# Four zs pairs beside the attention, silu written with tanh and a GpSimd multiply, split queries stored by row

## The chip, the core and the metric

One NeuronCore of a Trainium2 chip runs the whole kernel. The metric is the device time of one launch in microseconds. Five instruction queues work side by side, each strictly in its own order: PE (TensorE, matrix products), DVE (VectorE), ACT (ScalarE), POOL (GpSimd) and SP (SyncE, which only issues DMAs here). An instruction waits for others through semaphores, and whatever stands behind it on its queue waits with it.

## What is computed

The reference is one layer of a hybrid encoder on 1024 tokens of width 1024, in float32, cut here to what matters:

```python
h = rmsnorm(x, norm_g)
q, k, v, za, u, vs, zs, gm = split(h @ w_in)
q, k = partial_rope(q), partial_rope(k)
a   = (window_sink_attention(q, k, v, sinks) * silu(za)) @ w_att_out
sgo = chunked_spatial_gating(gelu(u), gelu(vs), ...)      # gelu(u) * (mixed + bias)
sgo = (sgo * silu(zs)) @ w_sg_out
ga, gs = split(sigmoid(gm + b_merge))
x = rmsnorm(x + (ga * a + gs * sgo) @ w_o, final_g)
```

The attention has 16 query heads and 2 key heads of 64 dimensions, a window of 128 frames in chunks of 64, and rotates the first 16 dimensions of each head. The change concerns `silu(zs)`, its product with the spatial gating's output, the rotation of q, and the order in which column groups of `h @ w_in` are computed.

## The kernel before

**Products.** Activations stand transposed: channels on the 128 partitions, tokens along the free dimension. Each float32 number is split into a high and a low part (`split`, L146: a copy on ACT makes `hi`, a subtraction on DVE makes `lo`), and a product is the sum of three matmuls, hi·hi, hi·lo and lo·hi. `gemm_pair` (L348) makes a pair of 128-channel groups `m` and `m+1` for all 1024 tokens with a seven-product scheme: seven calls of `product` (L331), 12 matmuls of 128x512 each. Their names in the profile are those of the activation forms: b11, t1, t2, b21, t3, b22, t4, in this order. Copies on ACT (L357, L361, L364) keep intermediate sums in tiles of the tag "x" (five buffers), additions on DVE (L369, L374, L378) finish three of the four 128x512 quarters there, and the fourth quarter is left in PSUM with its sign turned. After each quarter `gemm_pair` calls `finish(i, half, q, src, sign)`, and between products it calls a `hook`, seven times a pair.

**Weights.** `jobs` (L408 to L417) lists the pairs in the order in which their weights are loaded, summed (four additions on DVE, L240 to L243, for jobs made by `pair_job`) and split; `split_next` does this a few products ahead of use. The list has to be in the order in which the pairs are computed. For some later jobs the sums are made in DRAM ahead of time by accumulating DMAs on POOL's queue (`early_job`, L294, and `o_sums`, L440).

**Stages.** After the normalisation and the vs projection come: four u pairs, with `mix` (L763) beside them, which makes the spatial gating's output, multiplies it by gelu(u) (L783) and stores it in `s1_dr`; one pair for k and v; four q pairs; the zs pair 0 beside the last rotation steps; the zs pairs 2, 4 and 6 and then eight pairs for the merge gates (gs, ga), all eleven beside the attention; then za, the two output projections and the last product.

**Queries.** For each quarter of q, `split_q` (L878) makes hi and lo scaled by -1/8 and stores them in `q_hl`, shaped (2, 1024, 1024): hi or lo, row, token. A row's 512 tokens of hi and of lo lie in two places of 2 KB. `rotate` (L932) loads the rotating rows back from `q_raw`, turns them and overwrites them in `q_hl` by four DMAs for each half of the rotation. `query_stage` (L1027) loads, for a group of heads and 128 tokens, hi and lo by one DMA each.

**The zs pairs.** `zs_pair` (L1047) collects the four quarters, and only after the whole pair does silu on ACT (L1064) for all four, one behind the other by manual dependencies and behind the last exp (`exps`), and then multiplies each by its part of `s1_dr` on DVE (L1074) and stores it in `s_dr`. The parts are loaded into two tiles: of tag "rot" and after the pair for pair 0, of tag "g" from the third hook on for the others. So the four "x" tiles of a pair stay taken until these stores have landed, and the next pair takes three more.

**The order of the work.** A scheduler places each engine's instructions in a fixed order from the written order and its own estimate of times; `after` (L156) adds order without a wait. `part_of_attention` (L1250) advances the attention at each hook by one or two parts (`PARTS`, nine parts to a pair, seven in the first pair). A part is one of: scores and softmax (`softmax_stage`, L1092: matmuls L1110, minimum L1118 and L1119 on DVE, exp L1123 and L1133 on ACT, scaling L1141 on DVE and L1143 on ACT), turning the weights (`weight_stage`, L1146: transposes L1154, casts and subtractions) and the product with the values (`value_stage`, L1178: matmuls L1195, L1201 on ACT, L1202 on DVE, a store by POOL, L1204).

Of the kernel before, what the change touches and what calls it, by code (L numbers as in the profile page):

```python
# [30 lines left out]
P = 128  # L31
# [21 lines left out]
def hybrid_tile(  # L53
# [709 lines left out]
    def mix(g, half, q):  # L763

        pm = bank("tp")
        for t in range(4):
            nc.tensor.matmul(  # L767
                pm[:, t * P : (t + 1) * P],
                xh[:, half * 4 + t, g * P : (g + 1) * P],
                bias[-1][1][:, g % 4, :],  # L770
                start=True,
                stop=True,
            )
        p3 = pm[:].rearrange("p (t i) -> p t i", t=4)
        nc.vector.scalar_tensor_tensor(
            p3,
            p3,
            lg_sb[:, g : g + 1],
            bias[-1][0][:, g % 4, :].unsqueeze(1).broadcast_to([P, 4, P]),
            op0=ALU.mult,  # L780
            op1=ALU.add,
        )
        nc.vector.tensor_mul(q[:], q[:], pm[:])  # L783
        put(s1_dr, g, half, q[:])

    def both():
# [103 lines left out]

    halves = [slice(half * 64, half * 64 + 64) for half in range(2)]

# [39 lines left out]
    def rotate(g, pause):  # L932
# [7 lines left out]
        def split_rows(src, j):  # L940
# [1 line left out]
                src,  # L942
                [
                    (
                        (halves[half], a),
                        q_hl[a].rearrange("(h d) t -> h d t", h=16)[
                            8 * g : 8 * g + 8, 8 * j : 8 * j + 8, half_of(half)
                        ],
                    )
                    for a in range(2)  # L950
                    for half in range(2)
                ],
            )
# [23 lines left out]
    for m in range(0, KC, 2):  # L977

        def finish(i, half, q, src, sign):
# [4 lines left out]
            split_q(q[:], [(slice(0, P), q_hl[:, rows, half_of(half)].rearrange("a p t -> p a t"))])  # L984

        if m == 2:
            steps_of_q.append(rope_tables())
# [39 lines left out]
    def query_stage(g, t, par):  # L1027
# [1 line left out]
            key_stage(g, t)  # L1029
        qt = mtile([P, 4, P], F32R, "q", 2, aheads)  # L1030
        for j in range(2):
            rows = q_hl[j].rearrange("(c r d) t -> r d c t", r=2, d=HD)[par]
            nc.sync.dma_start(
                qt[j * HD : (j + 1) * HD].bitcast(F32), rows[:, 4 * g : 4 * g + 4, t * P : (t + 1) * P]
            )
        return qt

    qT = []
    exps = []

    def first_loads():
        for n in range(2):
# [1 line left out]
            yield  # L1044


    def zs_pair(m, hook, *place, ahead_by=0):  # L1047
        quarters, fetched, hooked = [], [], [0]

        def fetch(i, half):  # L1050
            fetched.append(get(s1_dr, m + i, half, *place))

        def step():
            hook()
            hooked[0] += 1
            if hooked[0] == ahead_by:
                for at in ((0, 0), (1, 1)):
                    fetch(*at)

        gemm_pair(hb, lambda *quarter: quarters.append(quarter), step)  # L1060

        first = None
        for i, half, q, src, sign in quarters:
            silu = nc.scalar.activation(q[:], src, AF.Silu, scale=sign)  # L1064
            first = first or silu
            if silu is not first:
                after(silu, first)
            elif exps:
                after(silu, exps[-1])
        for i, half, q, src, sign in quarters:  # L1070
            if not fetched:
                fetch(i, half)
            g = fetched.pop(0)
            nc.vector.tensor_mul(q[:], q[:], g[:])  # L1074
# [17 lines left out]
    def softmax_stage(g, t, par, qt):  # L1092
# [40 lines left out]
        exps.append(nc.scalar.activation(es[:], es[:], AF.Exp))  # L1133
# [123 lines left out]
        for _ in range(1 if first else PARTS[of_pair[0] % 7]):  # L1257
            next(parts, None)

    for m in range(2, KC, 2):  # L1260
        zs_pair(m, lambda: part_of_attention(m == 2), 2, ahead_by=3)
    for dst in (gs_dr, ga_dr):
        for m in range(0, KC, 2):
            gemm_pair(hb, rest(dst, m), part_of_attention)
    for _ in parts:
        pass
# [436 lines left out]
```

## Time and profile before

| what | value |
|---|---|
| median of 3 runs | 928.03 us (928.03 to 928.74) |
| the profiled execution's own time | 928.07 us |
| its span in the trace | 926.3 us, so 1.77 us lie around it |
| DVE busy over the span | 690.2 us |
| ACT busy over the span | 530.2 us |
| POOL busy over the span | 126.8 us |
| mean granted TensorE clock | 0.997 of full speed |

The profile names an engine, a source line, the tile written and the tiles read, the shape, and the duration. In a timeline row the first number is the start in us from the start of the span and the second the duration. What stands in square brackets is the idle time of that engine just before, and what ended it. In the table of stretches each row is a stretch of the span; after its length stand the busy times of the engines in it, with instruction counts in brackets, then the granted clock, the busy share of the DMA engines and GB/s. A busy PE is not PE at its peak: matmuls of one product start every 0.227 us, although each is shown with some 0.39 us.

### The profile page before, as it was taken

The numbers are of one execution on the slowest core, as the hardware profiler recorded it, in microseconds if no ns is written. First come the engines' busy times: TensorE is split into PE (matmuls) and PEld (weight loads), VectorE is DVE, ScalarE is ACT, GpSimd is POOL, SyncE is SP. The second block draws the span as 40 slices with busy tenths as digits, with TensorE's granted clock in tenths as the row PEclk, the third lists the DMA queues.
The fourth block names the chain that finished last, engine by engine and source line by source line (L and its number), as shares of the span: only waits on it lengthen the run. The fifth ranks groups of instructions, "written<-read, shape, count | busy, mean of one in ns | idle before, by whom it ended". The sixth has DMA issues, their size and how long they took to land.

```text
span 926.3 us, 13222 instructions
## 1 busy us (share of the span) xinstructions
PE 906.1 (98%) x4337; PEld 751.3 (81%) x4337; DVE 690.2 (75%) x1243; ACT 530.2 (57%) x1056; POOL 126.8 (14%) x189
## 2 busy tenths in 40 slices
PE   8999999999999989999999999999999999999996
PEld 5888888888888778778888888888887887888885
DVE  6874776656678678888878888746498589579996
ACT  7852433334444468887766676744475475467443
POOL 0002222213011001101111121001100111210012
PEclk9999999999999999999999999999999999999998
DMA  7328778887788777778787779779669765998632
GB/s 261 137 89 210 215 195 180 157 161 219 240 286 262 216 242 200 214 212 232 188 228 258 234 168 262 209 263 324 212 197 330 257 196 157 289 316 283 207 114 114
DMA packets 128972, 202.23 MB, mean 218 GB/s; under 512 B 12456, under 2 KB 60840, under 8 KB 128904
## 3 DMA queue, kind: packets, MB, share of 16 engines
q1 hardware_dynamic: 109752, 148.69, 49.1%
q0 software_dynamic: 19008, 52.44, 24.0%
q8 instruction: 34, 0.56, 0.2%
q14 instruction: 34, 0.28, 0.1%
q10 hardware_dynamic: 144, 0.26, 0.1%
HBM read 144.59 MB, written 86.11 MB: 249 GB/s over the span
## 4 chain that ended last, share of the span: by engine, by line
PE 74%; DVE 11%; DMA 7%; ACT 3%; issue 3%; SPq 1%; DVEq 0%; ACTq 0%
PE ps_mm L339 31%; PE ps_o L339 22%; PE ps_mm L595 4%; DVE wl L154 3%; PE ps_sc L339 2%; PE ps_tp L339 2%; PE ps_sc L1110 2%; PE ps_o L1195 2%; PE ps_tp L1154 2%; DMA wr<-in_w_dram 1%; PE ps_tp L564 1%; PE ps_sc L564 1%; PE ps_o L564 1%; PE ps_mm L564 1%; PE ps_tp L767 1%
## 5 line engine op out<-in xcount | busy, mean ns | idle before, releaser
L153 ACT CAST wh<-s 128x1024 fp32r<-128x1024 f32 (+1 forms) x78 | 78.2, 1005 | 95.3 <-PE ps_mm L339 44.7
L154 DVE TENSOR_TENSOR wl<-wr,wh 128x1024 fp32r<-128x1024 f32 (+1 forms) x80 | 75.7, 947 | 56.4 <-ACT wh L153 55.5
L153 ACT CAST wh<-wr 128x1024 fp32r<-128x1024 f32 (+1 forms) x80 | 66.3, 830 | 79.8 <-PE ps_mm L339 37.8
L154 DVE TENSOR_TENSOR wl<-s,wh 128x1024 fp32r<-128x1024 f32 (+1 forms) x78 | 90.9, 1166 | 12.1 <-ACT wh L153 12.1
L339 PE MATMUL ps_o<-T_b22h,wh 128*128 128x512 f32 x148 | 58.8, 398 | 1.7 <-ACT x L361 1.7
L339 PE MATMUL ps_o<-T_t1h,wh 128*128 128x512 f32 x148 | 59.2, 400 | 0.3 <-ACT wh L153 0.2
L339 PE MATMUL ps_o<-T_b22l,wh 128*128 128x512 f32 x148 | 57.8, 391 | 0.0
L339 PE MATMUL ps_o<-T_b22h,wl 128*128 128x512 f32 x148 | 57.8, 390 | 0.0
L339 PE MATMUL ps_o<-T_t1h,wl 128*128 128x512 f32 x148 | 57.7, 390 | 0.0
L339 PE MATMUL ps_o<-T_t1l,wh 128*128 128x512 f32 x148 | 57.7, 390 | 0.0
L339 PE MATMUL ps_mm<-T_b11h,wl 128*128 128x512 f32 x140 | 54.8, 392 | 2.1 <-DVE wl L154 2.1
L339 PE MATMUL ps_mm<-T_t4h,wh 128*128 128x512 f32 x140 | 55.2, 394 | 1.5 <-DVE x L374 0.8
L339 PE MATMUL ps_mm<-T_t2h,wh 128*128 128x512 f32 x140 | 54.9, 392 | 1.3 <-ACT x L357 1.2
L339 PE MATMUL ps_mm<-T_t3h,wh 128*128 128x512 f32 x140 | 55.4, 396 | 0.2 <-ACT x L364 0.2
L1123 ACT ACTIVATE pr<-ps_sc,sm 128x192 f32<-128x192 f32 (+2 forms) x128 | 50.9, 409 | 8.1 <-DVE sm L1119 7.1
L339 PE MATMUL ps_mm<-T_b11h,wh 128*128 128x512 f32 x140 | 55.0, 393 | 0.0
L339 PE MATMUL ps_mm<-T_t4h,wl 128*128 128x512 f32 x140 | 54.7, 391 | 0.0
L339 PE MATMUL ps_mm<-T_t3h,wl 128*128 128x512 f32 x140 | 54.7, 390 | 0.0
L339 PE MATMUL ps_mm<-T_b11l,wh 128*128 128x512 f32 x140 | 54.6, 390 | 0.0
L339 PE MATMUL ps_mm<-T_t2h,wl 128*128 128x512 f32 x140 | 54.6, 390 | 0.0
L339 PE MATMUL ps_mm<-T_t4l,wh 128*128 128x512 f32 x140 | 54.5, 390 | 0.0
L339 PE MATMUL ps_mm<-T_t2l,wh 128*128 128x512 f32 x140 | 54.5, 390 | 0.0
(352 smaller groups left out, 2403.9 us busy)
## 6 DMA issues: line engine op xcount, KB each, us to landing
wr<-in_w_dram SPq DMA_DIRECT2D x86, 256.0 KB
sums<-in_w_dram POOLq DMA_DIRECT2D x20, 512.0 KB, 5.6
s<-sums SPq DMA_DIRECT2D x20, 512.0 KB
s_dr<-x SPq DMA_DIRECT2D x32, 256.0 KB
q_hl<-qhl SPq DMA_DIRECT2D x16, 512.0 KB
q<-q_hl SPq DMA_DIRECT2D x64, 128.0 KB
wr<-in_w_dram SPq DMA_DIRECT2D x14, 512.0 KB
y_dr<-x POOLq DMA_DIRECT2D x28, 256.0 KB, 6.6
```

Source lines behind the costliest of these rows:

```text
L153: nc.scalar.copy(hi, src)
L154: return nc.vector.tensor_sub(lo, src, hi.bitcast(F32))
L339: nc.tensor.matmul(acc, lt, rt, start=fresh and k == 0 and n == 0, stop=k == 3 and n == 2, skip_group_check=True,)
L564: mm = nc.tensor.matmul(acc, lt, rt, start=k == 0 and n == 0, stop=k == KC - 1 and n == 2)
L595: nc.tensor.matmul(acc[:], lt, rt, start=k == 0 and n == 0, stop=k == KC - 1 and n == 2)
L767: nc.tensor.matmul(pm[:, t * P : (t + 1) * P], xh[:, half * 4 + t, g * P : (g + 1) * P], bias[-1][1][:, g % 4, :], start=True, stop=True,)
L1110: nc.tensor.matmul(sc[:, i, k0:], q_of[:, c, i * P : (i + 1) * P], kt[:, f, k0:], start=f == 0, stop=f == 1,)
L1123: nc.scalar.activation(held_in[c, i], sc[:, i, lo:hi], AF.Exp, bias=nmax[:, c, i : i + 1], scale=-1.0, accum_out=sums[:, c, i : i + 1],)
L1154: nc.tensor.transpose(dst, pr[:, i, block * P : block * P + width], ident[:])
L1195: nc.tensor.matmul(po[:, cs], lt, rt, start=n == 0, stop=n == len(terms) - 1)
```

## The change

- The job list moves the first gs pair (`W_SG`, m = 0) ahead of the zs pairs. The gs pair 0, with the plain `rest` finish (L462), now stands beside the rotation; the four zs pairs, then gs 2, 4 and 6 and the four ga pairs stand beside the attention: eleven pairs, as before.
- `silu(z) * s1` is written as `(tanh(z/2) + 1) * (z * s1/2)`. The factor 0.5 goes into the multiplication that makes s1: L783, a two-tensor multiplication, becomes a scalar-tensor-tensor instruction.
- `zs_pair` handles each quarter as soon as it is there. For three quarters GpSimd multiplies `src` into the loaded part `g`; for the fourth, which lies in PSUM, DVE does it. Then ACT makes tanh in place over the quarter, DVE adds one and multiplies by `g`, and the result is stored. The tanh writes over what GpSimd reads, so it waits for GpSimd. Two parts are loaded at the pair's first hook, and each finish loads one more, into two tiles of tag "g".
- The manual order of silu behind exp (`exps`) is gone.
- `q_hl` becomes (row, half of the tokens, hi or lo, 512), so that a row's hi and lo lie side by side in 4 KB. A half of the rotation stores by two DMAs instead of four.

```diff
     q_raw = scratch("q_raw")
-    q_hl = scratch("q_hl", (2, D, S))
+    q_hl = scratch("q_hl", (D, 2, 2, HALF))
...
-    for base, step in ((W_U, 1), (W_Q, 0), (W_ZS, 1), (W_SG, 2), (W_ATT, 2)):
+    ALL = range(0, KC, 2)
+    for base, step, ms in ((W_U, 1, ALL), (W_Q, 0, ALL), (W_SG, 2, ALL[:1]), (W_ZS, 1, ALL), (W_SG, 2, ALL[1:]), (W_ATT, 2, ALL)):
...
-        nc.vector.tensor_mul(q[:], q[:], pm[:])
+        nc.vector.scalar_tensor_tensor(q[:], q[:], 0.5, pm[:], op0=ALU.mult, op1=ALU.mult)
...
         for at, dst in places:
-            nc.sync.dma_start(dst, hl[at].bitcast(F32))
+            nc.sync.dma_start(dst, hl[at].rearrange("p a t -> p (a t)").bitcast(F32))
...
-            rows = q_hl[j].rearrange("(c r d) t -> r d c t", r=2, d=HD)[par]
+            rows = q_hl[:, t // 4, j].rearrange("(c r d) t -> r d c t", r=2, d=HD)[par]
...
+    steps_of_q += [rotate(1, 1), first_loads()]
+    gemm_pair(hb, rest(gs_dr, 0), part_of_q)
+    stage.close()
...
+        def finish(i, half, q, src, sign):
             g = fetched.pop(0)
-            nc.vector.tensor_mul(q[:], q[:], g[:])
+            if sign < 0:
+                nc.vector.scalar_tensor_tensor(g[:], src, sign, g[:], op0=ALU.mult, op1=ALU.mult)
+            else:
+                nc.gpsimd.tensor_tensor(g[:], src, g[:], op=ALU.mult)
+            nc.scalar.activation(q[:], src, AF.Tanh, scale=0.5 * sign)
+            nc.vector.scalar_tensor_tensor(q[:], q[:], 1.0, g[:], op0=ALU.add, op1=ALU.mult)
             put(s_dr, m + i, half, q[:])
-
-    steps_of_q += [rotate(1, 1), first_loads()]
-    zs_pair(0, part_of_q, 5, "rot")
-    stage.close()
+            fetch()
+
+        gemm_pair(hb, finish, step)
...
-    for m in range(2, KC, 2):
-        zs_pair(m, lambda: part_of_attention(m == 2), 2, ahead_by=3)
-    for dst in (gs_dr, ga_dr):
-        for m in range(0, KC, 2):
+    for m in ALL:
+        zs_pair(m, lambda: part_of_attention(m == 0))
+    for dst, ms in ((gs_dr, ALL[1:]), (ga_dr, ALL)):
+        for m in ms:
             gemm_pair(hb, rest(dst, m), part_of_attention)
```

More of the change, by code (lines that the diff above doesn't have):

```diff
@@ L944, in split_rows @@
                     (
[L945 to L948, printed above, removed]
+                        halves[half],
+                        q_hl[:, half].rearrange("(h d) a t -> h d (a t)", h=16)[8 * g : 8 * g + 8, 8 * j : 8 * j + 8],
                     )
-                    for a in range(2)
                     for half in range(2)
@@ L983, in finish @@
             rows = slice((m + i) * P, (m + i + 1) * P)
-            split_q(q[:], [(slice(0, P), q_hl[:, rows, half_of(half)].rearrange("a p t -> p a t"))])
+            split_q(q[:], [(slice(0, P), q_hl[rows, half].rearrange("p a t -> p (a t)"))])
         if m == 2:
@@ L1044, in first_loads, with zs_pair, fetch @@
             yield
[L1047 to L1051, printed above, removed]
+    steps_of_q += [rotate(1, 1), first_loads()]
+    gemm_pair(hb, rest(gs_dr, 0), part_of_q)
+    stage.close()
+    def zs_pair(m, hook):
+        quarters = [(0, 0), (1, 1), (0, 1), (1, 0)]
+        fetched, hooked = [], [0]
+        def fetch():
+            if quarters:
+                i, half = quarters.pop(0)
+                fetched.append(get(s1_dr, m + i, half, 2))
         def step():
@@ L1055, in step @@
             hooked[0] += 1
[L1056 to L1072, printed above, removed]
-            g = fetched.pop(0)
-            nc.vector.tensor_mul(q[:], q[:], g[:])
+            if hooked[0] == 1:
+                fetch()
+                fetch()
+        def finish(i, half, q, src, sign):
+            g = fetched.pop(0)
+            if sign < 0:
[4 more added lines that the diff above has]
+            nc.vector.scalar_tensor_tensor(q[:], q[:], 1.0, g[:], op0=ALU.add, op1=ALU.mult)
             put(s_dr, m + i, half, q[:])
-    steps_of_q += [rotate(1, 1), first_loads()]
-    zs_pair(0, part_of_q, 5, "rot")
-    stage.close()
+            fetch()
+        gemm_pair(hb, finish, step)
     stage = ExitStack()
@@ L1132, in softmax_stage @@
         nc.vector.tensor_add(es[:], sk.unsqueeze(1).broadcast_to([P, 2, 2]), nmax[:])
-        exps.append(nc.scalar.activation(es[:], es[:], AF.Exp))
+        nc.scalar.activation(es[:], es[:], AF.Exp)
         nc.vector.tensor_add(es[:], es[:], sums[:])
@@ L1258, in part_of_attention @@
             next(parts, None)
-    for m in range(2, KC, 2):
-        zs_pair(m, lambda: part_of_attention(m == 2), 2, ahead_by=3)
-    for dst in (gs_dr, ga_dr):
-        for m in range(0, KC, 2):
+    for m in ALL:
+        zs_pair(m, lambda: part_of_attention(m == 0))
+    for dst, ms in ((gs_dr, ALL[1:]), (ga_dr, ALL)):
+        for m in ms:
             gemm_pair(hb, rest(dst, m), part_of_attention)
```

5 lines of the change are left out of this document (1 added, 4 removed).

## The prediction

> **What bounds the kernel now.** I began with the page: span, engines.
>
> ```profile
> span 926.3 us, 13222 instructions
> PE 906.1 (98%) x4337; PEld 751.3 (81%) x4337; DVE 690.2 (75%) x1243; ACT 530.2 (57%) x1056; POOL 126.8 (14%) x189
> ```
>
> PE is taken all the time, so a change that takes no matmul away can only gain where matmuls start late. The second view is the table of stretches, cut at the first b11 matmul of each pair.
>
> ```profile
> 297.08:318.10 21.02, 20.13 (x88) 15.98 (x86) 13.94 (x24) 10.79 (x16) 0.00 (x0) 1.00 0.73 229
> 318.10:345.72 27.62, 25.06 (x126) 20.17 (x125) 20.51 (x54) 15.94 (x50) 0.00 (x0) 1.00 0.73 233
> 345.72:373.30 27.58, 26.83 (x146) 22.64 (x145) 22.84 (x50) 22.63 (x57) 3.56 (x4) 1.00 0.77 210
> 373.30:401.00 27.70, 26.65 (x145) 22.14 (x144) 23.89 (x55) 23.25 (x59) 4.99 (x6) 1.00 0.85 224
> 401.00:429.07 28.07, 27.54 (x147) 22.37 (x145) 23.75 (x56) 22.86 (x59) 3.33 (x4) 1.00 0.81 221
> ...
> 506.44:532.58 26.14, 26.14 (x147) 22.62 (x146) 21.55 (x51) 18.64 (x54) 2.36 (x4) 1.00 0.69 220
> 532.58:558.71 26.13, 26.13 (x147) 22.61 (x145) 21.51 (x51) 18.61 (x54) 5.00 (x6) 1.00 0.82 180
> 259.00:278.04 19.04, 19.04 (x85) 15.77 (x84) 15.18 (x26) 9.14 (x14) 4.39 (x8) 1.00 0.82 272
> ```
>
> The rows are, in order: the pair beside the last rotation (zs 0), the first pair beside the attention (zs 2), zs 4, zs 6, gs 0 (which carries the silu of zs 6); then two undisturbed pairs beside the attention (ga 0 and 2) and one undisturbed pair without it (a q pair). Attention pairs with nothing in their way take 26.13 to 26.14 us, a bare pair takes 19.04. The clock is 1.00 in all of them. So the five pairs in question take 21.02 + 27.62 + 27.58 + 27.70 + 28.07 = 131.99 us. Without their waits they would take 19.04, then 25.06 for the first attention pair (it has seven attention parts instead of nine; I take its PE busy time), then three times 26.13: 122.5 us. **At most about 9.5 us, 1.0% of the kernel, lie in the stretch that the change touches.** The clearest late matmuls there, from the PE timeline:
>
> ```profile
> 315.20 0.50 PE L339 MATMUL ps_mm<-T_t4h,wh 128*128 128x512 f32 x1 [0.78 <-DVE x L374]
> ...
> 331.40 0.50 PE L339 MATMUL ps_o<-T_b22h,wh 128*128 128x512 f32 x1 [1.73 <-ACT x L361]
> ...
> 381.70 0.50 PE L339 MATMUL ps_mm<-T_t2h,wh 128*128 128x512 f32 x1 [0.91 <-ACT x L357]
> ```
>
> Next I asked each of them what its releaser had waited for. The largest one, at 331.40, from DVE, SP and ACT:
>
> ```profile
> 321.62 2.40 SPq L198 DMA_DIRECT2D rot<-s_dr  x4
> 326.67 0.69 DVE L1074 TENSOR_TENSOR x<-x,rot 128x512 f32<-128x512 f32 x1 [5.22 <-DMA rot<-s_dr]
> 327.39 3.42 SPq L455 DMA_DIRECT2D s_dr<-x  x4
> 330.75 0.60 ACT L361 ACTIVATE x<-ps_o 128x512 f32<-128x512 f32 x1 [3.36 <-DMA s_dr<-x]
> 331.73 1.28 ACT L1123 ACT_TABLE_LOAD   x1 [0.39 <-DMA s_dr<-x]
> ```
>
> The reader is to see a chain: zs 0 loads its four s1 parts only after the rotation, DVE waits 5.22 us for them, the stores start at 327.39, and only when one has landed is an "x" tile free for ACT's copy at 330.75, which PE needs. At 381.70 the copy L357 comes late because it stands on ACT behind a silu block with its table loads:
>
> ```profile
> L1064 ACT ACT_TABLE_LOAD x4 | 5.1, 1283 | 0.1
> L1123 ACT ACT_TABLE_LOAD x4 | 5.1, 1283 | 0.4 <-DMA s_dr<-x 0.4
> ...
> L1064 ACT ACTIVATE x<-x 128x512 f32<-128x512 f32 x12 | 7.1, 625 | 0.6 <-DVE x L374 0.5
> ```
>
> **The change part by part.** *The gs pair beside the rotation.* Its quarters are stored directly, so the chain from 321.62 to 331.40 goes: no s1 part is loaded in this pair, four plain stores take the place of four loads and four late stores on SP, and one copy with a sign on ACT (some 0.6 us) that of four silu and a table load. That frees 2.56 us of waiting in the first attention pair (27.62 - 25.06). What is late next there is the softmax's own start, with the table load of 1.28 us that the first exp still needs; I leave 0.5 us for it, bounds 0 and 2. The rotation pair's other wait stays:
>
> ```profile
> 312.05 0.69 DVE L959 TENSOR_TENSOR rot<-rot,tab 128x512 f32<-128x512 f32 x1 [0.78 <-DMA rot<-q_raw]
> ...
> 314.47 0.68 DVE L374 TENSOR_TENSOR x<-x,ps_mm 128x512 f32<-128x512 f32 x1
> ```
>
> The subtraction L374, which PE waits for at 315.20, stands behind four rotation instructions, and these behind the load of q_raw. The built program of the changed kernel has them in the same order. I leave 1.2 of the 1.98 us that this pair is longer than 19.04, bounds 0.2 and 2.
>
> *Queries by row.* The same bytes; a rotation half has two DMAs instead of four, so this pair and the one before lose eight issues on SP of about 0.6 us each (2.40 for four at 321.62), on a queue that is not the bound. No trace shows a 4 KB row, so its price lies between landing earlier than before (the rotation's loads, and L374 behind them, come earlier: a gain of at most the 1.2 us above) and, if the reads with the doubled row pitch are slower, a query load that holds PE; I take nothing, since bytes and issue order stay.
>
> *Silu by tanh.* The changed program's ACT order has 8 table loads instead of 15: none stands between exp and tanh. A zs pair's ACT work falls by 2 x 1.283 = 2.57 us; tanh is a pass over the same 128x512, taken at silu's 625 ns (the trace has no tanh; I bound it by L361's 0.60 us and by twice silu, 1.25; the upper end would give back 2.5 of ACT's 2.57 us). ACT goes from about 23 to 20.5 us of 26, so the late L357 copies should go. The "x" tiles are given back quarter by quarter, as in the gs and ga pairs, which show no such wait.
>
> *DVE's bill.* The rows:
>
> ```profile
> L775 DVE SCALAR_TENSOR_TENSOR ps_tp<-ps_tp,lg_sb,bias 128x512 f32<-128x512 f32 x16 | 11.9, 753 | 0.6 <-PE ps_tp L767 0.6
> ...
> L1074 DVE TENSOR_TENSOR x<-x,g 128x512 f32<-128x512 f32 x12 | 8.2, 691 | 7.1 <-DMA g<-s_dr 3.7 <-ACT x L1064 3.2
> ```
>
> A zs pair now has four instructions like L775 (0.75) and one from PSUM, taken as long as L1074 (0.69): 3.69 us, against 4 x 0.69 = 2.76 before. On top of a plain attention pair (21.5) that is 25.2 us of DVE in 26.13, 96%. That is the tightest place of the changed kernel. Making s1 with the factor 0.5 costs 16 x (0.75 - 0.69) = 1.0 us more on DVE beside the u pairs, where I count nothing: only the store to s1_dr follows, and beside pairs without attention DVE has room (15.18 of 19.04 us in the q pair); without that cover it would be the 1.0 us.
>
> *GpSimd's multiply.* Three per zs pair, twelve in all.
>
> ```profile
> L1546 POOL TENSOR_TENSOR g<-bq,bq 128x512 f32<-128x512 f32 x2 | 2.6, 1305 | 4.3 <-DVE bq L1541 3.9 <-issue 0.4
> ```
>
> At 1.3 us each this is 3.9 us on an engine that is busy for 3 to 5 us of such a pair. Behind it wait ACT's tanh, so every exp and cast behind tanh, and POOL's own DMAs (paced sums and the attention's stores, both off the path). Does it slow DVE? The only place of this trace where DVE and such a multiply are close:
>
> ```profile
> 9.00 1.28 POOL L582 TENSOR_TENSOR T_t1l<-T_t3h,T_t1h 128x512 fp32r<-128x512 f32 x1 [7.56 <-ACT T_t1h L581]
> ...
> 9.44 0.69 DVE L554 TENSOR_TENSOR T_b11l<-ps_tp,T_b11h 128x512 fp32r<-128x512 f32 x1 [0.31 <-ACT T_b11h L553]
> ...
> 10.87 1.22 DVE L154 TENSOR_TENSOR T_t1l<-T_t3h,T_t1h 128x1024 fp32r<-128x1024 f32 x1
> ```
>
> A DVE instruction with one input in PSUM ran at its normal length beside it; the next one with both inputs in SBUF began after it had ended. So the trace bounds the price of a multiply for DVE between 0 and its own 1.28 us, and does not decide. The Trainium skill, "SBUF — State Buffer", section "SBUF: two separate sides", speaks against this change: it says that GpSimd and a VectorE instruction with two SBUF inputs take one shared pair of ports in turn, each holding it for its whole length. The rows above agree with it without proving it; by it the sum would move towards the slow rival below.
>
> *Loading s1.* Two tiles, so the third part is loaded after the first finish, two products ahead of its use.
>
> ```profile
> 409.55 0.42 SPq L198 DMA_DIRECT2D g<-s_dr  x1
> ...
> 413.96 0.69 DVE L1074 TENSOR_TENSOR x<-x,g 128x512 f32<-128x512 f32 x1 [1.75 <-DMA g<-s_dr]
> ```
>
> A load takes 413.96 - 409.55 = 4.4 us from issue to use. A finish (add 0.69, multiply 1.3, tanh 0.63, DVE 0.75, with gaps some 4.5 us) plus SP's store and load plus 4.4 makes about 10 us; two products with the attention between them are 2/7 of 26.13, 7.5 us. So the third part may hold POOL and ACT, and the fourth DVE, by 0 to 2.5 us. PE bears some of it: the scores of one part are used two parts later.
>
> So a zs pair beside the attention lies between 26.13 (all hidden) and more than the 27.7 of now. I take the middle, 26.9. **Sum:** 20.2 + 25.6 + 3 x 26.9 = 126.5 against 131.99, a gain of 5.5 us. From the profiled execution's 928.07 us (926.3 of span and 1.77 around it) that gives 922.6; the median of the runs is 928.03, the same, and I write 922.5.
>
> **The rivals.** *Everything hides:* 19.4 + 25.1 + 3 x 26.15 = 123.0, gain 9.0, 919. For it: PE's order in the changed program is as regular in the zs pairs as in the ga pairs, where before scores and products were cut into pieces. Against it: DVE at 96%.
>
> *DVE was the bound all along:* ACT's relief is worth nothing in three zs pairs, which stay at 27.7. For it: DVE ran 23.75 to 23.89 us in the two longest. Then 20.2 + 25.6 + 83.1 = 128.9, gain 3.1, 925.
>
> *Nothing is left:* the zs pairs go to 28.2 to 29, 926.2 to 929.9. That also holds the case that the change doesn't do what it says, if tanh brought its table loads back (4 pairs x 2.57 us on ACT).
>
> *GpSimd holds DVE, slower:* in zs 2, 4 and 6 each multiply holds DVE. Held in full it is 25.2 + 3 x 1.28 = 29.0 us of DVE a pair, and with one wait of 1.75 us for the fourth s1 part 30.8; held for 1 us each and with that wait, 29.95. At 29.95 the three pairs make 89.9, with 26 for the first and 20.2: 136.1, a loss of 4.1, 932. In full, with 27 for the first, 139.6: 936. It decides from (131.99 - 20.2 - 25.6) / 3 = 28.7 us a pair, 3.5 us more than DVE's own 25.2. Against it: about half of DVE's instructions read PSUM, and only the others can meet the multiply.
>
> **How the numbers follow.** Forecast (920.4 to 924.2, likeliest 922.5): 0.40. Everything hides (917.5 to 920.4): 0.15. DVE the bound (924.2 to 926.2): 0.19. Nothing left: 0.12. Slower: 0.14. About 0.2%, 1.9 us, is what a measurement can tell here from no change, so faster, below 926.2, has 0.74, same 0.12, slower, above 929.9, 0.14. The range from 918 to 930 leaves out the slow rival and the edge of the fast one, some 0.17.
>
> **What would show it.** No ACT_TABLE_LOAD ahead of tanh, and one ahead of the first exp. No wait of L361 for an s_dr store in the first attention pair, which should be near 25.6 us. In the zs pairs: DVE busy near 25 us; if the ports are shared, DVE instructions with two SBUF inputs start when a POOL multiply ends. Multiplies much longer than 1.3 us, or waits of PE for DVE in these pairs, would speak for the slow rival. The forecast is wrong if the first attention pair stays above 27 us, or the pairs after zs 6 are longer than 26.2 because DVE's arrears are paid there.

## The result and the profile after

The changed kernel takes **935.39 us** (934.36 to 936.48, 4 runs), the kernel before 928.03 (927.27 to 928.74, 4 runs): a ratio of 1.0071, 95% interval 1.0053 to 1.0088. It is slower by some 7 us; forecast were 922.5 us in a range of 918 to 930. The profiled execution took 936.48 us with a span of 934.7, so 8.4 us of span have to be found.

The page of the kernel after, to be held against that of before:

```profile
span 934.7 us, 13231 instructions
...
PE 908.7 (97%) x4337; PEld 753.3 (81%) x4337; DVE 696.4 (75%) x1247; ACT 521.2 (56%) x1049; POOL 147.0 (16%) x201
```

PE has gained 2.6 us of busy time with the same matmuls, and the rest of the 8.4 us is waiting. DVE has 6.2 us more, POOL 20.2 more, ACT 9.0 less. The table of stretches of the kernel after is cut where each pair's first product begins to run through; one or two of its matmuls can stand some us ahead of the cut. The columns: start and end; length; busy time of PE, PEld, DVE, ACT, POOL; granted clock; DMA share; GB/s.

```profile
296.91:319.54 22.63, 19.60 (x86) 15.88 (x85) 15.14 (x25) 8.13 (x12) 0.00 (x0) 1.00 0.74 234
319.54:347.89 28.35, 26.25 (x127) 21.72 (x126) 17.73 (x48) 16.69 (x49) 4.74 (x3) 0.94 0.67 209
347.89:375.39 27.50, 26.59 (x144) 22.29 (x142) 24.03 (x53) 19.50 (x55) 7.33 (x7) 1.00 0.75 205
375.39:405.44 30.05, 27.71 (x147) 22.64 (x146) 24.91 (x56) 20.57 (x56) 10.79 (x10) 1.00 0.82 215
405.44:434.19 28.75, 27.31 (x147) 22.55 (x145) 25.70 (x56) 20.38 (x56) 7.08 (x7) 1.00 0.80 212
434.19:463.58 29.39, 27.27 (x146) 22.54 (x145) 24.95 (x57) 20.21 (x56) 6.27 (x7) 1.00 0.74 188
```

The rows are gs 0 beside the rotation, zs 0, 2, 4 and 6, and gs 2. The first five make 137.28 us against 131.99 of before, 5.3 more. The sixth, gs 2, carries no silu any more and still takes 29.39, where before's gs 2 took 26.18: 3.2 us of arrears. Together they are the loss; all other pairs are as before within 0.4 us. ACT has become idler (19.5 to 20.6 us a pair from zs 2 on, 22.6 to 23.3 before), as forecast. DVE has become busier. In the row of zs 0 the granted clock is 0.94: part of its 28.35 us is this clock (experiment 1).

Of the late matmuls shown of before, that at the end of the rotation has grown, and the one that waited for L361 is gone; the first softmax now starts late. From PE's and DVE's timelines:

```profile
316.65 0.50 PE L339 MATMUL ps_mm<-T_t4h,wh 128*128 128x512 f32 x1 [3.03 <-DVE x L374]
...
327.48 0.62 DVE L1115 TENSOR_REDUCE sm<-ps_sc 128x2 f32<-128x128 f32 x2 [5.59 <-DMA q_hl<-qhl]
```

Where PE waits in zs 4, and what it waits for, from the timelines of the four engines of the kernel after (start, duration; in brackets the idle time before and what ended it):

```profile
394.83 0.69 DVE L369 TENSOR_TENSOR x<-x,ps_o 128x512 f32<-128x512 f32 x1
395.44 1.22 DVE L154 TENSOR_TENSOR wl<-wr,wh 128x1024 fp32r<-128x1024 f32 x1
395.66 2.15 POOL L1070 TENSOR_TENSOR g<-x,g 128x512 f32<-128x512 f32 x1 [1.73 <-issue]
397.84 0.63 ACT L1071 ACTIVATE x<-x 128x512 f32<-128x512 f32 x1 [4.53 <-POOL g L1070]
398.50 0.69 DVE L1072 SCALAR_TENSOR_TENSOR x<-x,g 128x512 f32<-128x512 f32 x1 [1.38 <-ACT x L1071]
399.12 0.15 DVE L1116 TENSOR_TENSOR sm<-sm,nsink_sb 128x2 f32<-128x2 f32 x1
399.30 0.42 ACT L1120 ACTIVATE pr<-ps_sc,sm 128x192 f32<-128x192 f32 x1 [0.22 <-DVE sm L1116]
400.27 0.75 PE L1107 MATMUL ps_sc<-k,q 128*128 128x256 f32 x4 [0.33 <-ACT pr L1120]
```

Read it from the top. DVE finishes the quarter (L369), and GpSimd may multiply. But DVE is already in its next instruction (L154, three operands in SBUF), and GpSimd's multiply takes 2.15 us: it ends 1.15 us after L154 has ended at 396.66, about the length that it has elsewhere. Tanh waits for it, DVE's last multiply waits for tanh and holds the softmax's L1116 behind it on DVE's queue, exp waits for that, and PE waits for exp to give back the score bank (0.33 us here, 3.9 us in the seven waits of this kind). The same chain runs the other way round too, GpSimd first:

```profile
404.47 1.28 POOL L1070 TENSOR_TENSOR g<-x,g 128x512 f32<-128x512 f32 x1 [2.01 <-DMA g<-s_dr]
404.64 2.19 DVE L154 TENSOR_TENSOR wl<-s,wh 128x1024 fp32r<-128x1024 f32 x1
```

Here L154, 1.22 us long above, takes 2.19: it does its work after the multiply has ended at 405.75. And in the summed waits of the kernel after (us in total, times, longest):

```profile
ACT x L1071 <- POOL g L1070: 21.4, 8, 4.7
...
POOL g L1070 <- DMA g<-s_dr: 9.8, 3, 4.5
...
PE ps_sc L1107 <- ACT pr L1120: 3.9, 7, 1.7
...
PE ps_tp L1151 <- DVE pT L154: 1.9, 2, 1.3
...
PE ps_o L1192 <- DVE x L369: 1.6, 4, 0.5
```

The first two cost time only as far as they end in waits of PE; the last three are PE's own.

So three theories stood against each other. **Wait:** tanh stands in ACT's order behind a GpSimd instruction, and DVE behind tanh. **Ports:** GpSimd's multiply and DVE's instructions with SBUF operands exclude each other (the shared pair of ports that the prediction speaks of). **Loads:** the third s1 part is loaded after the first finish and comes late. Rivals outside: DVE's own work of nearly a whole pair, the queries stored by row, the exchange of the pairs.

### The profile page after: what moved, and what is told of

It is laid out like the page before. It is cut to its first block, busy times and chain, and to the rows that moved or that the text cites. A ratio compares the mean times of both kernels' runs of the same rounds, so it can differ in the third digit from the quotient of the medians.

```text
span 934.7 us, 13231 instructions
## 1 busy us (share of the span) xinstructions
PE 908.7 (97%) x4337; PEld 753.3 (81%) x4337; DVE 696.4 (75%) x1247; ACT 521.2 (56%) x1049; POOL 147.0 (16%) x201
## 4 chain that ended last, share of the span: by engine, by line
PE 74%; DVE 12%; DMA 5%; issue 4%; ACT 2%; SPq 1%; POOL 1%; DVEq 0%; POOLq 0%; ACTq 0%
PE ps_mm L339 31%; PE ps_o L339 23%; PE ps_mm L596 4%; PE ps_sc L339 2%; PE ps_tp L339 2%; PE ps_sc L1107 2%; DVE wl L154 2%; PE ps_o L1192 2%; DMA g<-s_dr 2%; PE ps_tp L768 2%; PE ps_tp L1151 2%; PE ps_tp L565 1%; PE ps_sc L565 1%; PE ps_o L565 1%; PE ps_mm L565 1%
## 5 line engine op out<-in xcount | busy, mean ns | idle before, releaser
L154 DVE TENSOR_TENSOR wl<-wr,wh 128x1024 fp32r<-128x1024 f32 (+1 forms) x80 | 75.7, 947 | 52.5 <-ACT wh L153 52.4
L154 DVE TENSOR_TENSOR wl<-s,wh 128x1024 fp32r<-128x1024 f32 (+1 forms) x78 | 91.9, 1178 | 12.5 <-ACT wh L153 12.2
```

What stands on the lines that cost most here:

```text
L154: return nc.vector.tensor_sub(lo, src, hi.bitcast(F32))
```

## The experiments

Each is five rounds against the kernel before on the same chip; the ratio is to that kernel (928.2 to 929.3 us in these sets), with its 95% interval.

**1. The old layout of the queries, all else of the change kept.**

```diff
-    q_hl = scratch("q_hl", (D, 2, 2, HALF))
+    q_hl = scratch("q_hl", (2, D, S))
```

> The changed kernel with the split queries stored as before (two rows of 2 KB, twice as many DMAs), everything else of the change kept. If the stores by row are what made the rotation pair (22.63 us) and the wait of the first softmax (5.59 us) late, 2.5 to 4 us come back: about 932, the rotation pair near 20.5 and the first attention pair near 26.5. If the layout costs nothing, as the prediction took it, the time stays within 1 us of 935.4.

933.72 us, ratio 1.0053 (1.0037 to 1.0068). Rotation pair 20.50 us, first attention pair 26.92, but the next four 28.35, 29.02, 29.72 and 28.78. By the medians the layout costs some 1.7 us, less than the 2.5 us expected at least; the intervals of this ratio and of the changed kernel's (1.0053 to 1.0088) overlap. It is not the main cause. The granted clock of the first attention pair is 1.00 here, and the same 127 matmuls are busy for 24.80 us, against 26.25 at 0.94 in the kernel after.

**2. Rows alone, on the kernel before** (the opposite edit).

> The kernel before with the split queries stored by row, nothing else. The changed kernel with the old layout took 933.7 against 935.4, so if that layout costs by itself, 929.5 to 931, with the pair beside the rotation above 22 us and the wait of the softmax or of L374 longer. If it costs only in the changed order, 928 to 929.

929.50 us, ratio 1.0010 (0.9999 to 1.0020): at the edge of what can be told. The pair beside the rotation was 24.42 us in its profile, an execution of 931.68 us, at a granted clock of 0.93. Over all profiles here the pair beside the rotation took 20.18 to 25.40 us in eight profiles with rows (mean 22.9) and 20.50 to 21.74 in twelve with the old layout (mean 21.2). The five above 23 us all show a granted clock of 0.93 in that pair. In seven of the eight with rows, and in three of the twelve with the old layout, the clock is at 0.89 to 0.94 in that pair or the next one; so part of the layout's price may be the clock's. What else differs, from SP's and ACT's timelines; first the kernel before:

```profile
295.42 2.37 SPq L889 DMA_DIRECT2D q_hl<-qhl  x4
...
301.62 0.67 ACT L883 ACTIVATE qhl<-x 128x512 fp32r<-128x512 f32 x1 [1.13 <-DMA q_hl<-qhl]
```

and the kernel after:

```profile
296.70 4.89 SPq L891 DMA_DIRECT2D q_hl<-qhl  x4
...
303.92 0.66 ACT L885 ACTIVATE qhl<-x 128x512 fp32r<-128x512 f32 x1 [3.16 <-DMA q_hl<-qhl]
...
310.31 0.69 DVE L957 TENSOR_TENSOR rot<-rot,tab 128x512 f32<-128x512 f32 x1 [1.63 <-DMA rot<-q_raw]
```

The four stores from 296.70 are two of a half of the rotation (256 KB each) and two of whole quarters (512 KB each). They occupy SP for 4.89 us. The same 1.5 MB took 3.37 us before: five stores in a row from 294.79 (3.00 us; the first line shows the last four) and a sixth at 299.93 (0.37). Why they stand longer by rows isn't shown. Then the last split of q waits 3.16 us for a store to free its tile, 1.13 before. The load of q_raw stands behind that split's store on SP, the rotation waits for it, and L374, on which PE waits, stands behind the rotation. In every run with the old layout the last split began between 301.2 and 302.3, in those with rows between 302.6 and 305.3.

**3. The exchange of the pairs alone, on the kernel before.**

```diff
-    zs_pair(0, part_of_q, 5, "rot")
+    gemm_pair(hb, rest(gs_dr, 0), part_of_q)
...
-    for m in range(2, KC, 2):
-        zs_pair(m, lambda: part_of_attention(m == 2), 2, ahead_by=3)
+    for m in ALL:
+        zs_pair(m, lambda: part_of_attention(m == 0), 2, ahead_by=3)
```

> The kernel before with one part of the change: the gs pair beside the last rotation, all four zs pairs beside the attention, with silu in one batch per pair, the DVE multiply and the query layout of before. By the rows of before: 20.5 for the rotation pair, 25.5 for the first attention pair, three zs pairs at 27.7, 28.1 for the gs pair that carries the last silu: 157.2 against 131.99 + 26.18 = 158.2 of before, so 926 to 928. If the zs pairs need the rotation's room instead (more of the attention beside a batch of silu), 929 or more.

934.54 us, ratio 1.0058 (1.0042 to 1.0075): a miss. The pair beside the rotation is no shorter (21.68 us), the first attention pair neither (27.86), and the arrears of four batches of silu are paid in gs 2, which takes 31.92 us. The granted clock is 0.94 in the first attention pair and 0.95 in gs 2, so not all of this is waiting. From the timelines of that kernel there:

```profile
445.69 0.69 DVE L1075 TENSOR_TENSOR x<-x,g 128x512 f32<-128x512 f32 x1 [4.05 <-DMA g<-s_dr]
...
448.23 0.50 PE L339 MATMUL ps_mm<-T_t3h,wh 128*128 128x512 f32 x1 [2.65 <-ACT x L364]
```

DVE stands 4.05 us for a late s1 part, and PE 2.65 us for a copy behind it.

**4. Tanh without the exchange** (zs 0 beside the rotation with a batch of silu, times 2 x the halved s1; zs 2, 4 and 6 by tanh): with rows, with the old layout, and with the old layout and tanh issued later (the last edit is that of experiment 6).

```diff
-    gemm_pair(hb, rest(gs_dr, 0), part_of_q)
+    quarters = []
+    gemm_pair(hb, lambda *quarter: quarters.append(quarter), part_of_q)
...
-    for m in ALL:
+    for m in ALL[1:]:
```

> The changed kernel with the pairs in the order of before: zs 0 beside the rotation (its silu in one batch, times twice the halved s1), the gs pair back behind zs 6; zs 2, 4 and 6 keep tanh and the GpSimd multiply, the queries are stored by row. If the exchange of the pairs is the main cause (alone it took the kernel before from 929.0 to 934.5), four to six us come back: 929 to 931. If tanh with its wait and the ports is the main cause, three such pairs are left of four and the time stays above 932.5.

> As the run without the exchange, with the old layout of the queries too: the kernel before with nothing but tanh and the GpSimd multiply in zs 2, 4 and 6. By the layout's 1 to 2 us: 927.5 to 929.5, no gain over before (928.7 to 929.0 in these runs), since the table loads saved on ACT are given back as waits for GpSimd. If the use of tanh is a gain once it isn't in four pairs in a row, 925 to 927.

> As the run before it, with tanh and what follows it issued one attention part later, as in the run that deferred it (931.75 against 935.4). If the waits of ACT behind GpSimd are what spends the table loads' gain, 924.5 to 927, faster than both kernels. If the ports or DVE's load spend it, 928 to 930.

934.38 us (ratio 1.0060, 1.0046 to 1.0074), 935.07 (1.0064, 1.0049 to 1.0079) and 930.17 (1.0020, 1.0009 to 1.0030). So the exchange, which costs 5.5 us with batches of silu, costs nothing once tanh is used: 933.72 with it against 935.07 without, both with the old layout, and 929.73 (experiment 6) against 930.17 with tanh issued later. Tanh as written costs 6 to 7 us by itself. The theory that the exchange is the cause fell here: each half of the change alone costs at least as much as both. In the run with the old layout the first attention pair is 30.08 us at a granted clock of 0.89, with the wait for s1 behind the rotation back in it (PE 2.42 us for L361); with the exchange it is 26.92 at 1.00. With tanh later both stand at 1.00, with 29.00 us without the exchange and 25.80 with it. That part of the forecast holds. Of the layout nothing shows in this pair of runs: 934.38 us with rows, 935.07 without.

**5. No multiply on GpSimd; the same multiply earlier; the multiply on DVE.**

```diff
-            else:
-                nc.gpsimd.tensor_tensor(g[:], src, g[:], op=ALU.mult)
```

In the second kernel the line goes to the load as `tensor_tensor(g[:], g[:], g[:])`; in the third DVE multiplies all four quarters.

> The changed kernel without GpSimd's twelve multiplies: three quarters of each zs pair get (1 + tanh) * s1 without the factor z. Tanh then waits for nothing but its input, and no GpSimd instruction uses SBUF beside DVE. If tanh's wait behind GpSimd, or the ports that GpSimd shares with DVE, make the zs pairs long (28.35, 27.50, 30.05, 28.75, and 29.39 for the pair after them), these fall to 26 to 26.5 and the time to 925 to 927. If DVE's own load of 25 us a pair is the bound, the pairs keep 27.5 to 29 and the time stays above 932, since DVE has the same instructions.

> GpSimd keeps its twelve multiplies of 128x512 with all operands in SBUF, but squares the s1 part as soon as that is loaded, instead of multiplying z by it (so the output lacks z and has s1 squared in three quarters of each zs pair): the use of the ports stays, tanh no longer waits for GpSimd. If the wait of tanh is the cause, the time is that of the run without multiplies within 1.5 us (925 to 928). If the ports are the cause, it stays at 932 to 936, and DVE instructions with two SBUF inputs beside the multiplies are as long as in the changed kernel.

> The changed kernel with the multiply of all four quarters on DVE, none on GpSimd. Per zs pair DVE gets three more passes of about 0.75 us, 27.2 us and more of work in a pair of 26.13. If DVE's load is the bound, every zs pair is over 28.5 us and the time above 937. If GpSimd's wait or ports cost more than 2.25 us a pair, it is faster than the changed kernel: 930 to 933, with DVE over 95% busy in the zs pairs.

929.73 us (ratio 1.0010, 1.0000 to 1.0021), 936.26 (1.0085, 1.0062 to 1.0109) and 935.23 (1.0069, 1.0053 to 1.0086). GpSimd's multiply with tanh's wait for it is worth 5.7 us, with rows and late loads still there. The first kernel met neither of its forecasts: zs 2 falls to 25.82 us, but zs 6 and gs 2 still take 28.93 and 28.54. Moved away from tanh it costs as much as before, which speaks for the ports. It is no clean proof: in that run DVE's last multiply waits for GpSimd instead (9.60 us in four waits). On DVE the multiply costs what it cost on GpSimd.

**6. Tanh and what follows it one attention part later,** with rows and with the old layout.

```diff
+            def tail():
-            nc.scalar.activation(q[:], src, AF.Tanh, scale=0.5 * sign)
+                nc.scalar.activation(q[:], src, AF.Tanh, scale=0.5 * sign)
...
+            tails.append(tail)
```

> The changed kernel with tanh, the last DVE multiply, the store and the next s1 load of each quarter issued one attention part later, behind that part's instructions on ACT and DVE; the GpSimd multiply stays where it is. Tanh then finds GpSimd done. If the wait of ACT in its order (21.4 us behind GpSimd in the four zs pairs) is the cause, these waits go and the time falls to 927 to 931. If the ports or DVE's load are the cause, it stays above 933; a later third load could make it longer still.

> The changed kernel with the old layout of the queries and the deferred tanh, the pairs exchanged as in the change. If the two add up (1.7 and 3.6 us of 935.4): 930. The difference to the run without the exchange is the price of the exchange with the tanh form at its best: 3 to 6 us if the fourth zs pair beside the attention costs by its work there, near 0 if it cost only through the waits that the other two edits took away.

931.75 us (ratio 1.0043, 1.0027 to 1.0060) and 929.73 (1.0015, 1.0006 to 1.0025): some 4 us back. The pairs from zs 2 to gs 2 are still at 27.3 to 29.1. This doesn't separate wait from ports, for it also moves the multiply's meetings with DVE.

**7. No late loads** (rows kept; two quarters multiply by what the tile still holds).

```diff
             put(s_dr, m + i, half, q[:])
-            fetch()
+            fetched.append(g)
```

> The changed kernel without the loads of the third and fourth s1 part of each zs pair: these quarters multiply by what the tile still holds, so half of s's output is wrong in value; every arithmetic instruction stays. If the late third load is what holds GpSimd, tanh and DVE (9.8 us of waits of GpSimd for it in the trace of the changed kernel), the zs pairs fall by 1 to 1.5 us each and the time to 928 to 931. If the use of the ports, DVE's load or the chain DVE, GpSimd, ACT, DVE itself is the cause, it stays above 933.

933.25 us (ratio 1.0055, 1.0042 to 1.0067): inconclusive, 2 us at most, and its pair beside the rotation was the longest of all, 25.40 us.

**8. The ladder.** From the old layout (933.72) the three suspects are taken away one after the other. All three kernels load one s1 part per pair, four instead of sixteen in all, and their multiplies read one tile instead of two (1.04 us alone, 1.28 in the kernel after), so that the first step holds more than the lateness of the loads. In the first, GpSimd multiplies aside, and tanh waits for it; in the second, nothing waits for it; in the third, it isn't there.

```diff
+                aside = mtile([P, HALF], F32, "g", 2, pool)
+                multiply = nc.gpsimd.tensor_tensor(aside[:], g[:], g[:], op=ALU.mult)
+                follow(multiply, term[0])
...
+            tanh = nc.scalar.activation(q[:], src, AF.Tanh, scale=0.5 * sign)
+            if sign > 0:
+                follow(tanh, multiply)
```

> As the run with the ports alone, with tanh waiting for GpSimd's multiply as in the changed kernel: the late loads are all that is missing against the old layout's 933.7. If the wait is the main price, 3 to 5 us above the run with the ports alone, at 930 to 933. If the ports are, within 1.5 us of it.

> As the run with one load and no GpSimd, but GpSimd multiplies the s1 part by itself into a spare tile, behind the same DVE add as in the changed kernel, and nothing waits for it: only the use of the ports comes back. If the ports are the main price, 3 to 5 us above the run without it, DVE's short instructions with two SBUF operands at 0.5 us and more. If the wait is the price, within 1.5 us of it.

> The changed kernel with the old layout, without GpSimd's multiply, and with one s1 load per zs pair, used for all four quarters (three quarters lack the factor z, and three use the wrong part of s1). Tanh waits only for DVE's add, nothing waits for a late load, nothing uses SBUF beside DVE but ACT. If these three are the whole loss, the zs pairs are at 25.5 to 26.5 and the time at 920 to 924. If DVE's and ACT's own work and their order are a bound too, as the run without GpSimd suggests (929.7 with rows, its last two pairs 28.9 and 28.5), 925 to 928.

| kernel | us | ratio to before, 95% | step |
|---|---|---|---|
| old layout | 933.72 | 1.0053 (1.0037 to 1.0068) | |
| late loads gone | 929.29 | 1.0004 (0.9995 to 1.0013) | 4.4 |
| tanh's wait gone too | 928.21 | 0.9996 (0.9986 to 1.0007) | 1.1 |
| the multiply gone too | 921.32 | 0.9919 (0.9906 to 0.9931) | 6.9 |

In this order the ports are the largest step and the loads the second; the wait's step is within what the intervals leave open. In the other order it looks different: experiment 5 takes multiply and wait away first, for 5.7 us, and from there to the ladder's end rows and late loads together are worth 8.4, some 6.7 for the loads if the rows cost 1.7. So both are causes, and which is the larger isn't shown. The stretches of the kernel with the ports alone (the pairs zs 2, 4, 6 and gs 2):

```profile
344.19:371.52 27.33, 26.66 (x143) 22.31 (x142) 25.12 (x53) 19.90 (x56) 7.63 (x8) 1.00 0.66 174
371.52:399.54 28.02, 27.23 (x147) 22.67 (x145) 26.14 (x56) 20.37 (x57) 8.99 (x9) 1.00 0.80 202
399.54:427.26 27.72, 27.02 (x146) 22.66 (x145) 26.08 (x56) 20.30 (x57) 7.38 (x7) 1.00 0.75 190
427.26:454.55 27.29, 26.71 (x146) 22.57 (x145) 25.27 (x57) 19.30 (x55) 4.98 (x6) 1.00 0.77 186
```

and of the kernel without the multiply (the rotation pair, then zs 0 to gs 2):

```profile
296.97:317.94 20.97, 20.12 (x87) 15.99 (x86) 13.78 (x24) 7.57 (x12) 0.00 (x0) 1.00 0.70 232
317.94:343.59 25.65, 24.25 (x126) 20.33 (x125) 19.03 (x49) 17.66 (x51) 0.00 (x0) 1.00 0.88 233
343.59:369.42 25.83, 25.83 (x144) 22.28 (x142) 23.33 (x54) 20.55 (x57) 3.46 (x4) 1.00 0.73 192
369.42:395.60 26.18, 26.18 (x147) 22.62 (x145) 24.27 (x56) 20.27 (x57) 4.99 (x6) 1.00 0.82 206
395.60:421.78 26.18, 26.18 (x147) 22.62 (x145) 24.01 (x56) 20.20 (x57) 3.34 (x4) 1.00 0.78 210
421.78:447.96 26.18, 26.18 (x147) 22.61 (x145) 23.88 (x55) 18.63 (x54) 4.97 (x6) 1.00 0.77 197
```

From zs 2 on PE is busy for the whole length here: from zs 4 the pairs stand at the 26.18 us of an undisturbed one. What DVE loses to the multiply can be read from its busy time: over the rotation pair and the five behind it 136.32 us with it against 128.30 without, 8.0 us for twelve multiplies, 0.67 each. The instances, from the timelines of the kernel with the ports alone:

```profile
362.01 1.22 DVE L154 TENSOR_TENSOR wl<-wr,wh 128x1024 fp32r<-128x1024 f32 x1
362.18 1.95 POOL L1083 TENSOR_TENSOR g<-g 128x512 f32<-128x512 f32 x1 [2.60 <-DVE x L369]
363.15 1.53 DVE L1086 SCALAR_TENSOR_TENSOR x<-x,g 128x512 f32<-128x512 f32 x1
...
396.79 1.38 DVE L1151 TENSOR_SCALAR pr<-pr,sm 128x192 f32<-128x192 f32 x2
397.02 1.04 POOL L1083 TENSOR_TENSOR g<-g 128x512 f32<-128x512 f32 x1 [0.75 <-DVE x L378]
```

The multiply starts inside L154 and waits for its end at 363.23; L1086 then waits for the multiply's, and takes 1.53 us. In the groups it is 894 ns on the mean:

```profile
L1086 DVE SCALAR_TENSOR_TENSOR x<-x,g 128x512 f32<-128x512 f32 x16 | 14.1, 894 | 0.0
```

against the kernel without the multiply:

```profile
L1074 DVE SCALAR_TENSOR_TENSOR x<-x,g 128x512 f32<-128x512 f32 x16 | 10.7, 684 | 0.0
```

**9. Three tiles for s1** (with the old layout and the deferred tanh; the room is taken from the attention's output tile "aT", one left of two).

> The run with the old layout and the deferred tanh (929.7), with three tiles for s1, so that three parts are loaded ahead; the room comes from the attention's output tile, of which one is left of two. If the late third load is what is left, 927 to 928.5, at best faster than the kernel before by 0.1%. If the ports or DVE's work are what is left, or the single output tile makes waits, 929 to 932.

941.88 us (ratio 1.0137, 1.0124 to 1.0150): PE waits 11.2 us for DVE writing that one tile. It says nothing on the loads.

**10. The multiply on DVE, its product in the tile that the fourth result gets later, and the next s1 load issued before tanh**; in the first kernel the softmax's scaling stands wholly on ACT too. Both compute the whole reference, with the pairs exchanged and the old layout.

```diff
-                nc.gpsimd.tensor_tensor(g[:], src, g[:], op=ALU.mult)
+                if not fourth:
+                    fourth.append(xtile())
+                nc.vector.tensor_mul(fourth[0][:], src, g[:])
+                g = fourth[0]
+                fetch()
```

> The changed kernel with the old layout, all multiplies on DVE and none on GpSimd, the product z * s1 of three quarters written to the tile that the fourth result gets later, so that the next s1 load is issued before tanh, and the softmax's scaling of both halves on ACT instead of one on DVE. DVE then has about 24.9 + 2.1 - 1.7 = 25.3 us of work in a pair of 26.18, ACT about 22.6. If ports and late loads were the loss, the pairs come near 26.5 and the time to 922 to 926, faster than both kernels. If the chain DVE, ACT, DVE itself makes the pairs long, 928 or more.

> The same without the move of the softmax's scaling: DVE has about 27.0 us of work in a pair, more than the 26.18 of an undisturbed pair. If DVE's work is then the bound, 27.0 to 27.5 a pair, 4 to 5 us above the run with the scaling on ACT; if it isn't, the same as that run within 1.5 us.

927.63 us (ratio 0.9980, 0.9971 to 0.9988) and 928.02 (0.9990, 0.9980 to 1.0000). The first is faster than both kernels, by 0.2% than before and by some 0.9% than after (0.9980 / 1.0071). Moving the scaling made no difference that can be measured, so the forecast of 4 to 5 us between them failed, and with it DVE's summed work as the bound. In the first kernel DVE is busy for 128.4 us over the rotation pair and the five behind it, as on the ladder's end (128.30), and the time is 6 us longer. What is left of the 6 us to the ladder's end was not told apart: in the first kernel the first attention pair is 28.75 us at a granted clock of 0.94, and the three zs pairs behind it 27.4 on the mean.

## Why the prediction was wrong, point by point

The profiled execution is 13.9 us above the 922.6 of the sum. By the terms of the sum: the pair beside the rotation 2.4 (22.63 for 20.2), the first attention pair 2.8 (28.35 for 25.6), the three zs pairs 5.6 (28.77 on the mean for 26.9), and 3.2 in gs 2, which had no term.

- **The bound, 9.5 us in five pairs: held.** Without multiply and late loads, in a kernel that leaves out part of the work, the five pairs take 124.81 us (floor 122.5), and the whole kernel 921.3.
- **The gs pair beside the rotation: right in its mechanism.** The wait of L361 for a store is gone, and the first attention pair comes to 25.65 us on the ladder's end, where 25.6 was forecast. In the kernel after it is 28.35. The pair beside the rotation was forecast at 20.2; the ladder's end has 20.97, and the kernel after, with rows, 22.63.
- **Queries by row at no cost: probably wrong**, by some 1.7 us, at the edge of the noise. The bytes stayed, and the same 1.5 MB of stores occupied SP for 4.89 us instead of 3.37.
- **Tanh: right.** 8 table loads instead of 15, and a tanh pass takes 627 ns, where silu's 625 was taken.
- **DVE's bill of 25.2 us: too high, and not a bound.** On the ladder's end the pairs hold 26.18 us with 24.0 to 24.3 us of DVE. The last multiply takes 684 ns, not 753, which is 0.3 us a pair of the difference.
- **GpSimd's multiply: the step that failed.** The price for DVE was bounded between 0 and 1.28 us and left undecided, and the zs pair was put at the middle of its range, 26.9 us. The runs show 0.67 us of DVE for each multiply and 6.9 us of the kernel for twelve. The bound held; the middle of the pair's range didn't follow from it. In the ladder's last step PE loses nearly what DVE loses (6.5 us more in the five attention pairs for 8.0 of DVE). That this is because DVE had no time to give is argued and not shown: the first kernel of experiment 10 has no more DVE time than the ladder's end and is 6 us slower. The row of before couldn't decide it: L154 began 0.59 us after the multiply had ended, and until 10.73 DVE had been busy with instructions that read PSUM.
- **The s1 loads, 0 to 2.5 us a pair: in the range, and missing in the sum.** They are part of the same failed step: 4.4 us for four pairs in the ladder, some 6.7 in the other order, with hardly room for them in 26.9. GpSimd's own waits for a part, 9.8 us in three and up to 4.5, went beyond the 2.5 forecast.
- **The arrears: named as a sign, missing in the sum.** The 3.2 us of gs 2 belong to the zs pairs. Both signs of a wrong forecast came: the first attention pair above 27 us (28.35) and a pair after zs 6 above 26.2 (29.39).
- **The rival "GpSimd holds DVE", 932 to 936 us: its mechanism was what happened, its time came out partly by luck.** It took 29.95 to 30.8 us for each of zs 2, 4 and 6, which took 28.77 on the mean, hardly more than its point of decision, 28.7; and it took 1 to 1.28 us for each hold, where the runs show 0.67. With its other terms, 28.77 would give some 929. The rest are the rotation pair, the first attention pair and the arrears, which it didn't have. "About half of DVE's instructions read PSUM" was no argument against it: each of the twelve multiplies in the run with the ports alone held at least one of the others or was held by it.
- Halving s1 beside the u pairs cost nothing, as said: those pairs are as long as before.

Left open: why the exchange costs 5.5 us with batches of silu and nothing with tanh. The late s1 part in gs 2 was seen; it was not taken away.

## What to carry to other kernels

Beside a DVE that is over nine tenths busy, an elementwise instruction on GpSimd with operands in SBUF was no free help here: charge DVE with the time for which it is held, not with zero or a middle. Before a change is given up or kept, take its suspects away one after the other in one ladder, and in a second order too, for the steps depend on the order: here two edits that each looked like the cause cost 5.5 and 6.9 us alone and 5.0 together. A pair behind the changed ones shows arrears, so the sum has to reach until the lengths are normal again.

## What the runs showed of the hardware

- A DVE instruction with its inputs in SBUF and GpSimd's multiply excluded each other for whole instructions, in both directions: 2.15 and 1.95 us for a multiply that began inside L154, 2.19 us for an L154 of 1.22 that began inside a multiply. An addition with one input in PSUM and the other in SBUF was not held: L1212 at 366.27 took 0.67 us beside the multiply from 366.42 to 367.46 of the run with the ports alone, and 684 ns on the mean with and without multiplies. The Trainium skill, "SBUF — State Buffer", section "SBUF: two separate sides", describes the shared pair of ports as an exclusive lock for the instruction that starts first; the rows agree with it.
- It also held an instruction with one tensor from SBUF and one factor per partition: two of L1151 took 1.38 us beside a multiply, and 0.32 each on the mean without it (322 ns for this shape in the ladder's last kernel).
- Fewer and larger stores were not cheaper to issue: 1.5 MB in four stores with rows of 4 KB took SP 4.89 us, the same in six with rows of 2 KB 3.37.
- In the kernel after, 3.03 us without a matmul beside the rotation were followed by a granted clock of 0.94 over the first attention pair; with 1.67 us there, in the ladder's first kernel, it stayed at 1.00, with 1.58, in the exchange alone, it was 0.94, and with 0.61, in the kernel with the multiply earlier, 0.94 too. No length at which the clock falls can be read from these.
